# First block of a two-block transformer: HGRN levels on half the queries, weight splits on VectorE, padding zeros on GpSimdE

## The chip, the cores and the metric

One Trainium2 chip, one of its cores. The metric is device time of one execution in microseconds (us); lower is better. Times of before: median of three runs. Engines: TensorE (PE; its weight loads PEld), VectorE (DVE), ScalarE (ACT), GpSimdE (POOL), and SyncE (SP), which issues most DMAs.

## The reference, cut to what matters

Two residual blocks over 512 tokens of 1024 features, all in float32. The first has three mixers side by side (stick-breaking attention with 8 heads, an HGRN recurrence with 4 heads, memory attention with 4 heads), an output product, and a mixture of 16384 small experts (PEER). The second has three dilated-window groups and a memory attention. The change is in the first block's mixers; in the second it touches one pair of weights. The HGRN recurrence of a head is

```
f = lb + (1 - lb) * sigmoid(f_logit);  k = 1 - f;  b = cumsum(log f)
score[t, s] = sum_d q[t, d] * exp(b[t, d] - b[s, d]) * k[s, d]      for s <= t
out = score @ v  +  (q * exp(b)) @ state;   state = exp(b_last) * state + (k * exp(b_last - b))^T @ v
```

## The kernel before

**Weights.** A float32 product is made of three products of a faster TensorE type. Each weight tile of 128 x 2048 (8 chunks of 128 input features by 256 outputs) comes by two DMAs as `w_raw`; ScalarE rounds each half to `w_hi` (L110), and a second engine makes the rest, `w_lo = w_raw - w_hi` (L111, two SBUF operands of 1024 elements a partition, called a split below). `mm_feat` (L124 to L126) and `mm_tok` (L134 to L136) multiply hi*hi, hi*lo, lo*hi. `w_hi` and `w_lo` have two buffers, `w_raw` three. `weight(..., nc.gpsimd)` puts the splits of the first block's projections (`feat`, `tok`, `mem_kv`: 15 weights, 30 splits) and of `mem_kv_2` (2 weights) on POOL; `w_out` and everything later use DVE, but for 16 splits of the first `scores` pass of PEER, which stay on POOL before and after.

**HGRN.** `hgrn_head` works on one head at a time, keys and queries with features on partitions, 512 tokens along the row. Within a chunk of 128 tokens the scores come level by level (L = 64, 32, ..., 1): in each group of 2L tokens the queries of the upper half meet the keys of the lower half, with decays taken from the middle of the group. Per level: two subtractions on DVE (L351, L352) into `hg_d`, one exponential on ACT (L353), zeros in the unused halves of `hg_qt` and `hg_kt` by POOL (L355, L356), two products on DVE (L357, L358), four 128 x 128 x 128 float32 products on PE (L342; each is two records in the trace) and one predicated copy of 128 x 512 into the scores `hg_sc` (L359). Seven levels, four heads: 28 of each.

**Other names.** `stick` is the stick-breaking attention: per block of keys `sb_a` (scores), `sb_sp` (softplus, L300), `sb_h`/`sb_l` (its split, L304), a cumulative sum on PE (L306 to L309, tile `att`), L311, an exponential, and the values (L317, tile `acc`). `zero_pads` (L233, L234) clears the unused halves of padded queries. `norm_rows` and `head_rms` form a mean square, then one power on POOL (L97), then a multiplication (L163 for rows, L321 and L526 for heads).

**Order.** A scheduler orders every engine's instructions at build time, from the program's order and data dependences; at run time each engine takes its own list strictly in order. The two stick halves and four HGRN heads are interleaved with the products of the projections, which are the work that PE has at hand while DVE works through the levels.

Of the kernel before, what the change touches and what calls it, by code (L numbers as in the profile page):

```python
# [9 lines left out]
F32 = mybir.dt.float32  # L10
# [6 lines left out]
OP = mybir.AluOpType  # L17
# [3 lines left out]
S, D, P = 512, 1024, 128  # L21
NB = S // P
# [65 lines left out]
class Body:  # L88
# [96 lines left out]
    def mem_kv(self, xt, kT, v, pool, wpool, psm, pst):  # L185

        nc = self.nc
        wk = self.weight("w_mem_kv", 0, wpool, 2, nc.gpsimd)
        wv = self.weight("w_mem_kv", 1, wpool, 2, nc.gpsimd)
        ks = []  # L190
        for b in range(2):
            ps = psm.tile([P, 512], F32, name="mm")
            self.mm_tok(ps[:, :256], wk, xt, b * P)
            r = self.head_rms(ps[:, :256], 4, pool)
            kn = pool.tile([P, 4, 64], F32, name="ma_a", bufs=2)
            nc.vector.tensor_tensor(kn, ps[:, :256].rearrange("p (h d) -> p h d", d=64),
                                    r[:, :, None].to_broadcast([P, 4, 64]), op=OP.mult)
            ks.append(kn.rearrange("p h d -> p (h d)"))
        for b in range(2):
            ps = psm.tile([P, 512], F32, name="mm")  # L200
            self.mm_tok(ps[:, :256], wv, xt, b * P)
            nc.vector.tensor_copy(v[:, b, :], ps[:, :256])
        for c in range(2):
            ps = pst.tile([P, 512], F32, name="tp")
            for b in range(2):
                nc.tensor.transpose(ps[:, b * P:(b + 1) * P], ks[b][:, c * P:(c + 1) * P], self.ident)
            nc.scalar.activation(kT[:, c, :], ps[:, :256], AF.Copy, scale=self.vec[:, V_MK:V_MK + 1])

    def mem_kv_2(self, xt, kT, v, wpool, psm):

        nc = self.nc
        wk, wv = (self.weight("w_mem_kv_2", i, wpool, 2, nc.gpsimd) for i in range(2))
        yield
        for c in range(2):
            ps = psm.tile([P, 512], F32, name="mm")
            self.mm_feat(ps[:, :256], wk, xt, c * P)
            nc.scalar.activation(kT[:, c, :], ps[:, :256], AF.Copy)
        for b in range(2):
            ps = psm.tile([P, 512], F32, name="mm")
            self.mm_tok(ps[:, :256], wv, xt, b * P)  # L220
            nc.vector.tensor_copy(v[:, b, :], ps[:, :256])
        yield
# [101 lines left out]
    def hgrn_head(self, h, q, k, vi, mixed, pool, phg, pst):  # L324

        nc = self.nc
        T = lambda n, bufs=1: pool.tile([P, S], F32, name=n, bufs=bufs)
        v4 = lambda t: t.rearrange("p (c q) -> p c q", c=4)
        b, d = T("hg_b", 2), T("hg_d", 2)
        lb, oml, moml = (self.lbv[:, n, h:h + 1] for n in range(3))  # L330
        nc.scalar.activation(d, k, AF.Ln, bias=lb, scale=oml)
        for c in range(NB):
            sl = slice(c * P, (c + 1) * P)
            nc.vector.tensor_tensor_scan(b[:, sl], self.rst, d[:, sl], 0.0, op0=OP.mult, op1=OP.add)
        nc.vector.tensor_scalar(k, k, moml, oml, op0=OP.mult, op1=OP.add)
        sc = T("hg_sc", 2)

        def scores(kt, qt):
            pd = phg.tile([P, 512], F32, name="hs")
            for c in range(NB):  # L340
                sl = slice(c * P, (c + 1) * P)
                nc.tensor.matmul(pd[:, sl], kt[:, sl], qt[:, sl], start=True, stop=True)  # L342
            return v4(pd)

        nc.vector.tensor_tensor(v4(sc), scores(k, q), self.ident[:, None, :].to_broadcast([P, 4, P]), op=OP.mult)
        for n, L in enumerate(LEVELS):
            bl = lambda t: t.rearrange("p (n l) -> p n l", l=2 * L)
            bb = bl(b)
            mid = bb[:, :, L - 1:L].to_broadcast([P, S // (2 * L), L])
            d = T("hg_d", 2)  # L350
            nc.vector.tensor_tensor(bl(d)[:, :, L:], bb[:, :, L:], mid, op=OP.subtract)  # L351
            nc.vector.tensor_tensor(bl(d)[:, :, :L], mid, bb[:, :, :L], op=OP.subtract)  # L352
            nc.scalar.activation(d, d, AF.Exp)  # L353
            qt, kt = T("hg_qt", 2), T("hg_kt", 2)
            nc.gpsimd.memset(bl(qt)[:, :, :L], 0.0)  # L355
            nc.gpsimd.memset(bl(kt)[:, :, L:], 0.0)  # L356
            nc.vector.tensor_tensor(bl(qt)[:, :, L:], bl(d)[:, :, L:], bl(q)[:, :, L:], op=OP.mult)  # L357
            nc.vector.tensor_tensor(bl(kt)[:, :, :L], bl(d)[:, :, :L], bl(k)[:, :, :L], op=OP.mult)  # L358
            nc.vector.copy_predicated(v4(sc), self.hmask[:, n, :][:, None, :].to_broadcast([P, 4, P]), scores(kt, qt))  # L359

        d = T("hg_d", 2)
        nc.vector.tensor_tensor(v4(d), v4(b)[:, :, P - 1:P].to_broadcast([P, 4, P]), v4(b), op=OP.subtract)
        nc.scalar.activation(d, d, AF.Exp)
        kt = T("hg_kt", 2)
        nc.vector.tensor_tensor(kt, d, k, op=OP.mult)
        nc.scalar.activation(b, b, AF.Exp)
        qd = T("hg_qt", 2)
        nc.vector.tensor_tensor(qd, b, q, op=OP.mult)
        vsl = slice(h // 2 * P, h // 2 * P + P)
# [54 lines left out]
    def first(self, cp, gp, xr):  # L424
        nc, tc, A = self.nc, self.tc, self.A
        with ExitStack() as es:
# [24 lines left out]
            def tok(i, dst):
                w = self.weight("w_in", i, wpool, 2, nc.gpsimd)
# [8 lines left out]
            def hgrn_in(pair):  # L461
# [2 lines left out]
                feat(6 + pair, both[:, 0])  # L464
                return both[:, 0], both[:, 1]

            vi = pool.tile([P, NB, 256], F32, name="hg_i")
            rows = []
            for n in range(2):
# [814 lines left out]
```

## Time and profile before

| | us |
|---|---|
| median of three runs | 1969.91 (1967.43 to 1970.49) |
| the profiled execution | 1971.19 |
| its span in the trace | 1969.4 |
| first block, to the last addition of `w_out` (L585) | about 393 |

The profiled execution is 1.3 us above the median; the trace covers all of it but 1.8 us. A wait "<- X" after an instruction names what ended the idle time of its engine just before it. Busy times of PE are modelled and overlap a little, so its waits are more telling than its share.

### The profile page before, as it was taken

What the parts mean: (1) busy time and instruction counts of PE and PEld (TensorE: products, weight loads), DVE (VectorE), ACT (ScalarE), POOL (GpSimd) and SP (SyncE); (2) the same over time, 40 slices, a digit from 0 to 9 for tenths busy, and PEclk for the clock granted to TensorE, in tenths of its full rate; (3) what the DMA queues carried; (4) which work ended last, traced back from release to release, by engine and by line L of the source; (5) the groups of instructions that cost most, each with busy time, mean ns of one, the idle gap of its engine ahead of it and who ended that gap; (6) DMA issues with size and microseconds to landing.
All of it is one profiled execution on the core that took longest, in us unless ns stands there. A gap on an engine that the chain in (4) does not pass through costs nothing.

```text
span 1969.4 us, 29893 instructions
## 1 busy us (share of the span) xinstructions
PE 1873.6 (95%) x11285; PEld 1703.4 (86%) x11285; DVE 1403.8 (71%) x2718; ACT 866.7 (44%) x1363; POOL 562.0 (29%) x479
## 2 busy tenths in 40 slices
PE   7899888989889989999999999999999799999998
PEld 6778787989889989999998999999998678889898
DVE  3387886369999979767876877787787675433563
ACT  4474745155569654333333433343333433443442
POOL 4323322070000000034443544455444332113100
PEclk9999998999999999999999999999999999999999
DMA  4211102454457686778999999989998775422221
GB/s 159 84 47 61 44 22 67 148 163 142 148 177 268 208 288 186 235 262 311 339 319 314 311 340 328 330 304 334 323 318 308 275 255 186 149 73 89 76 65 54
DMA packets 150769, 399.25 MB, mean 203 GB/s; under 512 B 12768, under 2 KB 62048, under 8 KB 147552
## 3 DMA queue, kind: packets, MB, share of 16 engines
q1 hardware_dynamic: 110688, 257.30, 39.4%
q0 software_dynamic: 39360, 137.94, 19.5%
q8 instruction: 88, 1.44, 0.3%
q10 hardware_dynamic: 576, 2.10, 0.3%
q14 instruction: 57, 0.47, 0.1%
HBM read 364.75 MB, written 30.41 MB: 201 GB/s over the span
## 4 chain that ended last, share of the span: by engine, by line
PE 59%; DVE 13%; issue 7%; DMA 6%; POOL 3%; ACT 2%; POOLq 0%; DVEq 0%; SPq 0%; ACTq 0%
PE o L720 20%; PE hp L624 7%; PE hp L626 7%; PE hp L625 7%; PE mm L134 3%; PE mm L136 3%; PE mm L135 3%; DVE w_lo L111 2%; DMA g_row<-peer_u,idx 2%; DMA g_row<-peer_v,idx 2%; DVE onehot L913 2%; DMA w_raw<-peer_v 1%; PE mm L124 1%; PE mm L125 1%; PE mm L126 1%
## 5 line engine op out<-in xcount | busy, mean ns | idle before, releaser
L110 ACT ACTIVATE w_hi<-w_raw 128x1024 fp32r<-128x1024 f32 x366 | 386.1, 1060 | 576.4 <-DMA w_raw<-peer_v 199.2
L111 DVE TENSOR_TENSOR w_lo<-w_raw,w_hi 128x1024 fp32r<-128x1024 f32 x316 | 384.4, 1219 | 103.3 <-ACT w_hi L110 97.3
L624 PE MATMUL hp<-xT_hi,w_hi 128*128 128x384 f32 x1024 | 350.2, 342 | 0.4 <-ACT act L630 0.4
L626 PE MATMUL hp<-xT_hi,w_lo 128*128 128x384 f32 x1024 | 347.6, 339 | 2.5 <-DVE w_lo L111 2.5
L625 PE MATMUL hp<-xT_lo,w_hi 128*128 128x384 f32 x1024 | 346.8, 339 | 0.0
L954 POOL DMA_INDIRECT g_row<-peer_u,idx x128 | 172.9, 1351 | 339.1 <-PE o L720 137.7
L720 PE MATMUL o<-w_hi,wl 128*128 128x512 f32 x768 | 240.2, 394 | 8.8 <-DVE wl L715 8.8
L720 PE MATMUL o<-w_hi,wh 128*128 128x512 f32 x768 | 241.1, 396 | 7.4 <-ACT wh L714 7.4
L720 PE MATMUL o<-w_lo,wh 128*128 128x512 f32 x768 | 239.5, 393 | 0.0
L954 POOL DMA_INDIRECT g_row<-peer_v,idx x128 | 174.0, 1359 | 222.6 <-PE o L720 149.2
L958 DVE SCALAR_TENSOR_TENSOR g_row<-g_row,kv 128x1024 f32<-128x1024 f32 x128 | 155.2, 1222 | 68.3 <-DMA g_row<-peer_u,idx 67.9
L624 PEld LDWEIGHTS hp<-xT_hi,w_hi 128*128 128x128 f32 x1024 | 193.2, 189 | 4.4 <-ACT act L630 0.8
L625 PEld LDWEIGHTS hp<-xT_lo,w_hi 128*128 128x128 f32 x1024 | 193.1, 189 | 3.6
L626 PEld LDWEIGHTS hp<-xT_hi,w_lo 128*128 128x128 f32 x1024 | 193.4, 189 | 3.1 <-DVE w_lo L111 3.1
L720 PEld LDWEIGHTS o<-w_hi,wl 128*128 128x128 f32 x768 | 145.5, 190 | 41.1 <-DVE wl L715 10.9
L720 PEld LDWEIGHTS o<-w_lo,wh 128*128 128x128 f32 x768 | 146.0, 190 | 32.0
L720 PEld LDWEIGHTS o<-w_hi,wh 128*128 128x128 f32 x768 | 144.4, 190 | 31.3 <-ACT wh L714 8.2
L963 DVE SCALAR_TENSOR_TENSOR x<-g_row,dots,x 128x1024 f32<-128x1024 f32 x100 | 128.3, 1283 | 48.9 <-DMA g_row<-peer_v,idx 48.5
L714 ACT ACTIVATE wh<-act 128x384 fp32r<-128x384 f32 x128 | 66.7, 522 | 203.7 <-PE o L720 192.6
L111 POOL TENSOR_TENSOR w_lo<-w_raw,w_hi 128x1024 fp32r<-128x1024 f32 x50 | 121.0, 2431 | 104.2 <-ACT w_hi L110 101.0
L125 PE MATMUL mm<-xT_lo,w_hi 128*128 128x256 f32 (+1 forms) x400 | 129.5, 324 | 0.0
L124 PE MATMUL mm<-xT_hi,w_hi 128*128 128x256 f32 (+1 forms) x384 | 127.2, 332 | 0.6 <-ACT xT_hi L153 0.6
(351 smaller groups left out, 3634.4 us busy)
## 6 DMA issues: line engine op xcount, KB each, us to landing
w_raw<-peer_uT SPq DMA_DIRECT2D x128, 512.0 KB
w_raw<-peer_v SPq DMA_DIRECT2D x128, 512.0 KB
w_raw<-w_in SPq DMA_DIRECT2D x54, 512.0 KB
gd<-stage SPq DMA_DIRECT2D x23, 1024.0 KB
gt<-gd SPq DMA_DIRECT2D x15, 1536.0 KB
w_raw<-w_query SPq DMA_DIRECT2D x32, 512.0 KB
w_raw<-w_out SPq DMA_DIRECT2D x16, 512.0 KB
w_raw<-w_mem_kv SPq DMA_DIRECT2D x8, 512.0 KB
```

Source lines behind the costliest of these rows:

```text
L110: nc.scalar.activation(hi[:, sl], raw, AF.Copy)
L111: eng.tensor_tensor(lo[:, sl], raw, hi[:, sl].bitcast(F32), op=OP.subtract)
L124: nc.tensor.matmul(ps, a, xh[:, kc, :], start=kc == 0, stop=False)
L125: nc.tensor.matmul(ps, a, xl[:, kc, :], start=False, stop=False)
L624: nc.tensor.matmul(ps, uh[:, kc, :], hi[:, kc, P:], start=kc == 0, stop=False)
L625: nc.tensor.matmul(ps, uh[:, kc, :], lo[:, kc, P:], start=False, stop=False)
L626: nc.tensor.matmul(ps, ul[:, kc, :], hi[:, kc, P:], start=False, stop=kc == KC - 1)
L714: nc.scalar.activation(wh, w, AF.Copy)
L720: last = nc.tensor.matmul(out[b][n], s_[:, sl], m_[:, n * 512:(n + 1) * 512], start=i == 0 and m_ is vh and s_ is wh, stop=i == NE - 1 and ...
L954: dma = nc.gpsimd.indirect_dma_start(out=u, out_offset=None, in_=A["peer_v" if k >= P else "peer_u"], in_offset=bass.IndirectOffsetOnAxis( ...
L958: nc.vector.scalar_tensor_tensor(u, u, 1.0, self.h2, op0=OP.mult, op1=OP.mult, accum_out=dots[:, c:c + 1])
L963: nc.vector.scalar_tensor_tensor(y, u, dots[:, c:c + 1], x, op0=OP.mult, op1=OP.add)
```

## The change

HGRN: the queries of the upper halves are packed into 256 columns (`hg_qt` of 128 x 256), the decays of queries and keys lie in the two halves of `hg_d`, the four products of a level move 64 columns instead of 128, and the predicated copy covers 256 elements (the late half of each group). `hg_kt` becomes two fixed tiles, cleared once; what a former level left in their other halves falls on rows that the mask doesn't copy. The 56 small memsets of POOL go. The last key product of a head is written over `hg_d`, and `hg_qe` takes the decayed queries. All 34 splits of POOL in `feat`, `tok`, `mem_kv` and `mem_kv_2` go to DVE (30 in the first block, 4 in the second). The padding zeros of the first stick half go from DVE to POOL.

```
-        wk = self.weight("w_mem_kv", 0, wpool, 2, nc.gpsimd)
+        wk = self.weight("w_mem_kv", 0, wpool)
...
-            nc.vector.tensor_tensor(bl(d)[:, :, L:], bb[:, :, L:], mid, op=OP.subtract)
-            nc.vector.tensor_tensor(bl(d)[:, :, :L], mid, bb[:, :, :L], op=OP.subtract)
+            nc.vector.tensor_tensor(half(d[:, :256]), bb[:, :, L:], mid, op=OP.subtract)
+            nc.vector.tensor_tensor(half(d[:, 256:]), mid, bb[:, :, :L], op=OP.subtract)
             nc.scalar.activation(d, d, AF.Exp)
-            qt, kt = T("hg_qt", 2), T("hg_kt", 2)
-            nc.gpsimd.memset(bl(qt)[:, :, :L], 0.0)
-            nc.gpsimd.memset(bl(kt)[:, :, L:], 0.0)
-            nc.vector.tensor_tensor(bl(qt)[:, :, L:], bl(d)[:, :, L:], bl(q)[:, :, L:], op=OP.mult)
-            nc.vector.tensor_tensor(bl(kt)[:, :, :L], bl(d)[:, :, :L], bl(k)[:, :, :L], op=OP.mult)
-            nc.vector.copy_predicated(v4(sc), self.hmask[:, n, :][:, None, :].to_broadcast([P, 4, P]), scores(kt, qt))
+            qt = pool.tile([P, 256], F32, name="hg_qt", bufs=2)
+            nc.vector.tensor_tensor(half(qt), half(d[:, :256]), bl(q)[:, :, L:], op=OP.mult)
+            kt = self.kts[n % 2]
+            nc.vector.tensor_tensor(bl(kt)[:, :, :L], half(d[:, 256:]), bl(k)[:, :, :L], op=OP.mult)
+            pd = phg.tile([P, 512], F32, name="hs")[:, :256]
+            for c in range(NB):
+                nc.tensor.matmul(pd[:, c * 64:(c + 1) * 64], kt[:, c * P:(c + 1) * P], qt[:, c * 64:(c + 1) * 64],
+                                 start=True, stop=True)
+            nm = P // (2 * L)
+            late = v4(sc).rearrange("p c (n l) -> p c n l", l=2 * L)[:, :, :, L:]
+            mask = self.hmask[:, n].rearrange("p (n l) -> p n l", l=2 * L)[:, :, L:]
+            nc.vector.copy_predicated(late, mask[:, None].to_broadcast([P, 4, nm, L]),
+                                      pd.rearrange("p (c n l) -> p c n l", c=4, l=L))
...
-                w = self.weight("w_in", i, wpool, 2, nc.gpsimd)
+                w = self.weight("w_in", i, wpool)
...
+            self.kts = [pool.tile([P, S], F32, name=f"hg_kt{n}") for n in range(2)]
+            for t in self.kts:
+                nc.gpsimd.memset(t, 0.0)
...
-            def stick_in(eng, g):
+            def stick_in(g):
...
-                self.zero_pads(qz, eng)
+                self.zero_pads(qz, nc.gpsimd)
```

The scheduler sets a new order. Three places of it, as the built programs have them. The first is DVE in the first levels of the third head. Before:

```order
L501 TENSOR_TENSOR hg_qf<-hg_qf,hg_d 128x512
L300 SCALAR_TENSOR_TENSOR sb_sp<-sb_a,sb_sp 128x512
L357 TENSOR_TENSOR hg_qt<-hg_d,hg_qf 128x4x64
L358 TENSOR_TENSOR hg_kt<-hg_d,hg_qf 128x4x64
L351 TENSOR_TENSOR hg_d<-hg_b 128x8x32
L304 TENSOR_TENSOR sb_l<-sb_sp,sb_h 128x512
L352 TENSOR_TENSOR hg_d<-hg_b 128x8x32
L351 TENSOR_TENSOR hg_d<-hg_b 128x16x16
L295 COPY sb_a<-att 128x512
L311 TENSOR_TENSOR sb_a<-sb_a,att 128x512
L357 TENSOR_TENSOR hg_qt<-hg_d,hg_qf 128x8x32
L345 TENSOR_TENSOR hg_sc<-hs,cst 128x512
```

And POOL, at the same place before (the two splits belong to the next weights):

```order
L97 TENSOR_TENSOR hr_r_1691<-rs_t,mhalf 128x4
L111 TENSOR_TENSOR w_lo<-w_raw,w_hi 128x1024 x2
L355 MEMSET hg_qt 128x16x16
L356 MEMSET hg_kt 128x16x16
L355 MEMSET hg_qt 128x32x8
L356 MEMSET hg_kt 128x32x8
```

DVE at the same place of the change (L349, L350 are the subtractions, L353 and L356 the products, L364 the predicated copy):

```order
L341 TENSOR_TENSOR hg_sc<-hs,cst 128x512
L300 SCALAR_TENSOR_TENSOR sb_sp<-sb_a,sb_sp 128x512
L353 TENSOR_TENSOR hg_qt<-hg_d,hg_qf 128x256
L356 TENSOR_TENSOR hg_kt_103<-hg_d,hg_qf 128x4x64
L353 TENSOR_TENSOR hg_qt<-hg_d,hg_qf 128x256
L356 TENSOR_TENSOR hg_kt_104<-hg_d,hg_qf 128x8x32
L349 TENSOR_TENSOR hg_d<-hg_b 128x256
L364 COPY_PREDICATED hg_sc<-hmask,hs 128x4x64
L304 TENSOR_TENSOR sb_l<-sb_sp,sb_h 128x512
L350 TENSOR_TENSOR hg_d<-hg_b 128x256
```

No split of a weight stands between this head's levels; the four of the two weights in question stand ahead of the head. In all four heads together, four splits stand between the first subtraction and the last predicated copy of a head (1, 2, 0 and 1). The second place is DVE at the start of the first stick half, before:

```order
L456 COPY sb_v<-mm 128x256 x4
L293 TENSOR_TENSOR sb_a<-att,cst 128x512
L300 SCALAR_TENSOR_TENSOR sb_sp<-sb_a,sb_sp 128x512
L304 TENSOR_TENSOR sb_l<-sb_sp,sb_h 128x512
L311 TENSOR_TENSOR sb_a<-sb_a,att 128x512
```

and in the change:

```order
L462 COPY sb_v<-mm 128x256 x4
L293 TENSOR_TENSOR sb_a<-att,cst 128x512
L111 TENSOR_TENSOR w_lo<-w_raw,w_hi 128x1024 x2
L300 SCALAR_TENSOR_TENSOR sb_sp<-sb_a,sb_sp 128x512
L304 TENSOR_TENSOR sb_l<-sb_sp,sb_h 128x512
L311 TENSOR_TENSOR sb_a<-sb_a,att 128x512
```

Two splits moved in between L293 and L300, where DVE waits for three passes of ACT over `sb_sp`. The third place is POOL at the program's start, before:

```order
L97 TENSOR_TENSOR rs<-rs_t,mhalf 128x1 x4
L111 TENSOR_TENSOR w_lo<-w_raw,w_hi 128x1024
L233 MEMSET sb_qz 64x2x512
L111 TENSOR_TENSOR w_lo<-w_raw,w_hi 128x1024
L234 MEMSET sb_qz 64x2x512
L111 TENSOR_TENSOR w_lo<-w_raw,w_hi 128x1024 x10
```

and in the change:

```order
L97 TENSOR_TENSOR rs<-rs_t,mhalf 128x1 x2
L233 MEMSET sb_qz 64x2x512
L97 TENSOR_TENSOR rs<-rs_t,mhalf 128x1
L234 MEMSET sb_qz 64x2x512
L97 TENSOR_TENSOR rs<-rs_t,mhalf 128x1
L233 MEMSET sb_qz 64x2x512
L234 MEMSET sb_qz 64x2x512
L97 TENSOR_TENSOR hr_r_612<-rs_t,mhalf 128x4
```

The first padding zeros now stand between the powers of the second, third and fourth block of rows, and no split is left among them. From the PEER stage on, the lists of all engines are the same but for the four splits of `mem_kv_2` and a few neighbours.

## Rows read from the trace of the kernel before

**Rows 1.** Page, busy time, share of the span and instructions of each engine.

```profile
PE 1873.6 (95%) x11285; PEld 1703.4 (86%) x11285; DVE 1403.8 (71%) x2718; ACT 866.7 (44%) x1363; POOL 562.0 (29%) x479
```

**Rows 2.** Waits of PE from 60 to 300 us: total us, times, longest.

```profile
PE hs L342 <- DVE hg_kt L358: 12.1, 5, 3.9
PE att L307 <- DVE sb_l L304: 3.4, 3, 1.6
PE acc L317 <- ACT sb_a L312: 2.2, 3, 1.4
PE att L306 <- ACT sb_h L303: 1.7, 1, 1.7
```

**Rows 3.** The same view from 300 to 345 us.

```profile
PE tp L530 <- DVE xrow L526: 2.8, 1, 2.8
```

**Rows 4.** Timeline around 220 us: start, us, engine, instruction, [idle before].

```profile
219.69 1.05 PE L342 MATMUL hs<-hg_qf 128*128 128x128 f32 x8
...
219.99 4.86 POOL L111 TENSOR_TENSOR w_lo<-w_raw,w_hi 128x1024 fp32r<-128x1024 f32 x2 [10.01 <-ACT w_hi L110]
220.26 2.38 DVE L357 TENSOR_TENSOR hg_qt<-hg_d,hg_qf 128x256 f32<-128x256 f32 x1
...
223.17 1.96 DVE L358 TENSOR_TENSOR hg_kt<-hg_d,hg_qf 128x256 f32<-128x256 f32 x1
...
225.28 0.91 PE L342 MATMUL hs<-hg_qt,hg_kt 128*128 128x128 f32 x6 [3.18 <-DVE hg_kt L358]
```

**Rows 5.** Groups of DVE by shape, 60 to 300 us: busy us, mean ns.

```profile
L359 DVE COPY_PREDICATED hg_sc<-hmask,hs 128x512 f32<-128x512 uint8 x28 | 20.5, 734 | 2.1 <-PE hs L342 2.0
L304 DVE TENSOR_TENSOR sb_l<-sb_sp,sb_h 128x512 fp32r<-128x512 f32 x20 | 17.2, 861 | 2.9 <-ACT sb_h L303 2.8
L357 DVE TENSOR_TENSOR hg_qt<-hg_d,hg_qf 128x256 f32<-128x256 f32 x28 | 17.0, 608 | 0.4 <-ACT hg_d L353 0.3
L358 DVE TENSOR_TENSOR hg_kt<-hg_d,hg_qf 128x256 f32<-128x256 f32 x28 | 16.6, 594 | 0.0
L300 DVE SCALAR_TENSOR_TENSOR sb_sp<-sb_a,sb_sp 128x512 f32<-128x512 f32 x20 | 15.6, 779 | 8.8 <-ACT sb_sp L299 8.6
L351 DVE TENSOR_TENSOR hg_d<-hg_b 128x256 f32<-128x256 f32 x28 | 13.9, 496 | 0.0
...
L352 DVE TENSOR_TENSOR hg_d<-hg_b 128x256 f32<-128x256 f32 x28 | 11.7, 417 | 0.0
...
L365 DVE TENSOR_TENSOR hg_kt<-hg_d,hg_qf 128x512 f32<-128x512 f32 x4 | 2.7, 676 | 0.0
```

**Rows 6.** Busy us (instructions) of the splits L111 from 60 to 300 us.

```profile
60.00:300.00 240.00, 0.00 (x0) 49.12 (x21) 0.99 0.16 50
```

**Rows 7.** Groups of DVE by shape, 300 to 395 us.

```profile
L111 DVE TENSOR_TENSOR w_lo<-w_raw,w_hi 128x1024 fp32r<-128x1024 f32 x8 | 9.6, 1220 | 1.3 <-ACT w_hi L110 1.3
```

**Rows 8.** Busy us of all engines and granted clock (PEclk) in two stretches.

```profile
60.00:300.00 240.00, 215.57 (x1321) 185.71 (x1319) 179.09 (x355) 135.65 (x222) 80.00 (x89) 0.99 0.16 50
300.00:340.00 40.00, 35.03 (x220) 30.16 (x221) 27.84 (x65) 22.65 (x54) 8.76 (x7) 0.87 0.22 72
```

**Rows 9.** Timeline of the start of the program.

```profile
10.48 0.75 DVE L163 TENSOR_SCALAR xrow<-sb_qz,rs 128x1024 f32<-128x1024 f32 x1 [0.67 <-POOL rs L97]
...
11.57 0.91 DVE L233 MEMSET sb_qz<- 64x1024 f32 x1 [0.27 <-DVE rs_t L96]
...
13.92 2.34 POOL L111 TENSOR_TENSOR w_lo<-w_raw,w_hi 128x1024 fp32r<-128x1024 f32 x1
...
14.32 2.49 DVE L163 TENSOR_SCALAR xrow<-sb_qz,rs 128x1024 f32<-128x1024 f32 x1
...
18.10 0.75 DVE L154 SCALAR_TENSOR_TENSOR xT_lo<-att,vec,xT_hi 128x512 fp32r<-128x512 f32 x1 [1.29 <-ACT xT_hi L153]
```

**Rows 10.** Timeline of PE, one run of half-precision products in the PEER stage.

```profile
601.55 0.64 PE L922 MATMUL g<-gated,onehot 128*128 128x128 f16 x8
```

**Rows 11.** Waits of ACT from 18 to 300 us.

```profile
ACT w_hi L110 <- PE mm L136: 13.5, 3, 8.5
```

More of the change, by code (lines that the diff above doesn't have):

```diff
@@ L187, in mem_kv @@
         nc = self.nc
-        wk = self.weight("w_mem_kv", 0, wpool, 2, nc.gpsimd)
-        wv = self.weight("w_mem_kv", 1, wpool, 2, nc.gpsimd)
+        wk = self.weight("w_mem_kv", 0, wpool)
+        wv = self.weight("w_mem_kv", 1, wpool)
         ks = []
@@ L211, in mem_kv_2 @@
         nc = self.nc
-        wk, wv = (self.weight("w_mem_kv_2", i, wpool, 2, nc.gpsimd) for i in range(2))
+        wk, wv = (self.weight("w_mem_kv_2", i, wpool) for i in range(2))
         yield
@@ L336, in hgrn_head @@
         sc = T("hg_sc", 2)
[L338 to L345, printed above, removed]
+        pd = phg.tile([P, 512], F32, name="hs")
+        for c in range(NB):
+            sl = slice(c * P, (c + 1) * P)
+            nc.tensor.matmul(pd[:, sl], k[:, sl], q[:, sl], start=True, stop=True)
+        nc.vector.tensor_tensor(v4(sc), v4(pd), self.ident[:, None, :].to_broadcast([P, 4, P]), op=OP.mult)
         for n, L in enumerate(LEVELS):
             bl = lambda t: t.rearrange("p (n l) -> p n l", l=2 * L)
+            half = lambda t: t.rearrange("p (n l) -> p n l", l=L)
             bb = bl(b)
@@ L350, in hgrn_head @@
             d = T("hg_d", 2)
-            nc.vector.tensor_tensor(bl(d)[:, :, L:], bb[:, :, L:], mid, op=OP.subtract)
-            nc.vector.tensor_tensor(bl(d)[:, :, :L], mid, bb[:, :, :L], op=OP.subtract)
+            nc.vector.tensor_tensor(half(d[:, :256]), bb[:, :, L:], mid, op=OP.subtract)
+            nc.vector.tensor_tensor(half(d[:, 256:]), mid, bb[:, :, :L], op=OP.subtract)
             nc.scalar.activation(d, d, AF.Exp)
-            qt, kt = T("hg_qt", 2), T("hg_kt", 2)
-            nc.gpsimd.memset(bl(qt)[:, :, :L], 0.0)
-            nc.gpsimd.memset(bl(kt)[:, :, L:], 0.0)
-            nc.vector.tensor_tensor(bl(qt)[:, :, L:], bl(d)[:, :, L:], bl(q)[:, :, L:], op=OP.mult)
-            nc.vector.tensor_tensor(bl(kt)[:, :, :L], bl(d)[:, :, :L], bl(k)[:, :, :L], op=OP.mult)
-            nc.vector.copy_predicated(v4(sc), self.hmask[:, n, :][:, None, :].to_broadcast([P, 4, P]), scores(kt, qt))
+            qt = pool.tile([P, 256], F32, name="hg_qt", bufs=2)
[3 more added lines that the diff above has]
+            pd = phg.tile([P, 512], F32, name="hs")[:, :256]
+            for c in range(NB):
+                nc.tensor.matmul(pd[:, c * 64:(c + 1) * 64], kt[:, c * P:(c + 1) * P], qt[:, c * 64:(c + 1) * 64],
[5 more added lines that the diff above has]
+                                      pd.rearrange("p (c n l) -> p c n l", c=4, l=L))
         d = T("hg_d", 2)
@@ L363, in hgrn_head @@
         nc.scalar.activation(d, d, AF.Exp)
-        kt = T("hg_kt", 2)
+        kt = d
         nc.vector.tensor_tensor(kt, d, k, op=OP.mult)
         nc.scalar.activation(b, b, AF.Exp)
-        qd = T("hg_qt", 2)
+        qd = T("hg_qe")
         nc.vector.tensor_tensor(qd, b, q, op=OP.mult)
@@ L451, in tok @@
             def tok(i, dst):
-                w = self.weight("w_in", i, wpool, 2, nc.gpsimd)
+                w = self.weight("w_in", i, wpool)
                 for b in range(NB):
@@ L552, in first @@
             tok(10, slabs(vi))
-            sb = stick_in(nc.vector, 0)
+            sb = stick_in(0)
             self.masks(cp, pool.tile([P, len(LEVELS) + 2, P], F32, name="hg_qf", bufs=1))
@@ L558, in first @@
             hgrn(0, *hin)
-            sb = stick_in(nc.gpsimd, 1)
+            sb = stick_in(1)
             hgrn(1, *hin)
```

## Prediction

> **What bounds the kernel now.** The page's first part comes first [rows 1]: PE is busy 95% of the span, DVE 71%, POOL 29%. So a gain has to come from PE's work or from PE's waits, not from busy time of DVE or POOL as such. The change lies in the first block, which ends near 393 us, so PE's waits there are read next, in the stretch of stick attention and HGRN heads from 60 to 300 us [rows 2]. Four kinds make 12.1 + 3.4 + 2.2 + 1.7 = 19.4 us, and one more of 2.8 us comes right behind [rows 3]: 22.2 us in all. Each ends on a DVE result, or on an ACT result that waited for one. In the same 240 us DVE is busy for 179.1 us, three quarters [rows 8], so it is not a shortage of DVE that PE waits for, but single late instructions.
>
> The timeline around 220 us shows why they are late [rows 4]. Two splits run on POOL from 219.99 to 224.85 us. L357, a product of 128 x 256 with both operands in SBUF, starts at 220.26 and lasts 2.38 us, until the first split ends; L358 starts at 223.17 and lasts 1.96 us, until the second ends. PE stood idle for 3.18 us and went on at 225.28 us. The means by shape say the same over the whole stretch [rows 5]: L352 (128 x 256, two SBUF operands) takes 417 ns, but L357 608, L358 594 and L351 496 at the same size; L365 (128 x 512) takes 676 ns, but L304 861 and L300 779. I read this as POOL's split and a DVE instruction with two SBUF operands not running side by side: the later one stands until the other is through. The stands add up to 20 x (0.861 - 0.676) + 20 x (0.779 - 0.676) + 28 x (0.608 - 0.417 + 0.594 - 0.417 + 0.496 - 0.417) = 3.7 + 2.1 + 12.5 = 18.3 us, beside PE's 19.4 us of waits: a stand on DVE goes through to PE nearly whole, since it strikes whichever instruction is next.
>
> **The change, part by part.** All sums are against the profiled execution, 1971.2 us.
>
> *The splits leave POOL.* The stands go with them, and with them PE's waits [rows 2, 3]: -22.2 us. At the least nothing is gained, if something else holds DVE as long (a rival below); more than the 22.2 is not there in these rows.
>
> *The splits arrive on DVE.* In the stretch 21 of them [rows 6] at 1.22 us [rows 7] make 25.6 us. On the other side DVE sheds the 18.3 us of stands, and the shorter predicated copies: no row has one of 256 elements, so I take the step between the unhindered products, 676 - 417 = 259 ns [rows 5], 28 times, 7.3 us (between nothing and half of 20.5, 10.3 us). 25.6 - 18.3 - 7.3 = 0: DVE has as much to do as before, in another order. What counts is who stands behind a split. By the new order, four of them stand between the levels of the four heads, where the next products of PE come from; the others stand ahead of a head, behind its last level, or where DVE has a wait for ACT anyway (8.6 us in L300's row [rows 5] are such waits). I let the four go through whole, 4 x 1.22 = +4.9 us; the bounds are 0 and all 21 of them, +25.6 us. Within the levels the packed operands have the same element counts for the subtractions and products, so they are taken at no change; POOL's 56 memsets were hidden behind other engines' work, and their end is taken at nothing.
>
> *The start.* The last block of rows, L163, lasted 2.49 us beside POOL's first split, an earlier one 0.75 [rows 9]: a stand of 1.74 us, with PE's first products behind it. I take 1.5 of it. Two zero-paddings of 0.91 us leave DVE's list between these rows and go to POOL, between its powers; that is a swap on the same chain and taken at nothing (bounds: 2 x 0.91 = 1.8 us either way). The first split now stands on DVE in front of the first L154, which waited 1.29 us for ACT anyway [rows 9], against 1.22 us. Sum -1.5 us, between -1.74 - 1.8 = -3.5 and +1.8.
>
> *The clock.* The granted clock is 0.99 in the long stretch and 0.87 from 300 to 340 us [rows 8]; the missing pulses are worth 0.01 x 240 + 0.13 x 40 = 2.4 + 5.2 = 7.6 us. The trace has the lower of the two levels, 1.2 GHz, in such stretches and 2.4 GHz else, and the fall comes behind gaps like that of [rows 4]. If the gaps go, part of it comes back; but 300 to 340 us has waits of its own (for powers and row sums) that stay. I take -3 us, between 0 and -7.6.
>
> *PE's products of the levels.* 112 products of 128 moving columns get 64. Each is two records, and eight records follow each other at 0.111 us (1.05 us for the eight at 219.69 us less a tail of about 0.28 us, by seven steps [rows 4]). If the step halves, 224 x 0.056 = 12.5 us of PE work go; if the weight load sets it, nothing does, since every product still loads 128 weights. No row has fewer than 128 moving columns. The nearest row with cheaper columns is L922, half precision at 128 columns: eight in 0.64 us [rows 10], about 0.06 us a step, but its weights are half precision too, so it does not tell the two apart. I take the bound nothing: the float32 steps in the trace never fall under this one. The Trainium skill has a rule that speaks against a gain here, in "TensorE: Matmul & The Clock Gate", section "LDWEIGHTS (loading the stationary operand)": a load takes the weight columns divided by 1.2, in ns, whatever is streamed behind it. By that rule, as an estimate, 128 columns cost 107 ns a record, next to the measured 0.111 us, and the term is 0; with the halved step of the same page's "Back-to-back issue gap" it would be -12.5 us.
>
> *The second block.* The four splits of `mem_kv_2` cost DVE 4 x 1.22 = 4.9 us where there is PE work of other weights at hand, and free it of at most as many stands of about 2 us. Taken at nothing, between +4.9 and -4 us, for want of a wait of PE that names them.
>
> Sum: -22.2 + 4.9 - 1.5 - 3 = -21.8 us, 1949.4 us for a profiled execution. That one stood 1.3 us over its median, so **1948 us**. The PEER stage behind starts when the last row of x is added and keeps its order, so it moves as a whole.
>
> **Rivals.**
>
> *DVE is simply the next to be late.* DVE's busy time does not change (25.6 us in, 25.6 us out). If splits hold PE as the stands did, us for us, only the start is gained: 1969.9 - 1.5 = 1968 us, no change. For it: from 100 to 300 us the levels are one chain on DVE, and a list in strict order can't let a level pass a split. Against: a quarter of DVE's time is free [rows 8], and the stands struck at random while the splits have places.
>
> *A split blocks its list.* A split on DVE waits for `w_hi`, and ACT can't write `w_hi` before PE is through with the weights of two tiles ago: that made ACT wait 13.5 us in three places, 8.5 us at the longest [rows 11]. On POOL nobody stood behind such a wait but memsets and powers; on DVE all levels do. 21 splits belong to about 11 weights. At the mean wait of 4.5 us each, on seven of them, 31.5 us come on top of 1948: 1980 us, slower. It decides from about 26 us, 2.3 us a weight. Against: the scheduler knows these dependences and puts the splits behind the products in question, and PE has to reach the same weights later anyway.
>
> *The halved products count.* 12.5 us less on PE, in a stretch that PE fills: 1935 us. It is the rule of the issue gap against that of the load, above.
>
> **How the numbers follow.** This kernel's measurement tells about 0.2%, 4 us, from no change (1966 to 1974 us). Chances: the forecast, 1938 to 1958 us, 0.55; the halved products or more clock, below 1938, 0.15; splits that cost PE most of what is gained, 1958 to 1974, 0.22, of which 0.12 lie under 1966; the blocked list, over 1974, 0.08. Faster 0.82, the same 0.10, slower 0.08. The range that leaves out about 2 in 10 reaches from 1929 (the halved products and the whole clock: 1948 - 12.5 - 4.6 = 1931, and a little of the start) to 1967 us; the likeliest case's own is 1938 to 1958.
>
> **What would show it.** Right: in the new trace L353, L356, L304 and L300 (its line before) have means near 0.42 and 0.68 us; PE's waits for them in the stretch to 300 us fall from 19 us to under 7; DVE's busy time there is the same within 5 us in a shorter stretch; the records of the level products still follow at 0.11 us. The first rival shows as PE waits of the same sum ending on the same DVE lines, now with L111 in front of them; the second as DVE idle in front of L111 for ACT; the third as a step near 0.06 us. The prediction is wrong if PE's waits go but the end of the block does not move, which would say that something other than PE's list bounds it.

## The result and the profile after

The changed kernel takes **1953.15 us** (median of 6 runs, 1947.34 to 1955.3), the kernel before 1969.51 us beside it (6 runs, 1967.12 to 1971.2). The ratio is 0.9926, 95% interval 0.9909 to 0.9944: 0.74% faster, 14.6 us by the ratio. The forecast was 1948 us with a range of 1929 to 1967. The profiled execution took 1954.04 us with a span of 1952.3, 17.1 us less than before.

The page of the changed kernel, busy time of each engine, answers to [rows 1]. POOL has lost its splits (562.0 to 474.5 us) and DVE has gained only 4.2 us, although it took them over:

```profile
PE 1867.4 (96%) x11285; PEld 1702.6 (87%) x11285; DVE 1408.0 (72%) x2750; ACT 864.5 (44%) x1363; POOL 474.5 (24%) x393
```

PE's waits from 60 to 300 us in the changed kernel (total us, times, longest) answer to [rows 2]. L359 is L342 before:

```profile
PE mm L134 <- DVE ma_a L196: 3.2, 1, 3.2
PE att L307 <- DVE sb_l L304: 2.2, 4, 0.9
...
PE hs L359 <- DVE hg_kt L356: 0.8, 1, 0.8
...
PE att L306 <- ACT sb_h L303: 0.3, 1, 0.3
PE acc L317 <- ACT sb_a L312: 0.3, 1, 0.3
```

The four kinds of [rows 2] made 19.4 us; the same four make 2.2 + 0.8 + 0.3 + 0.3 = 3.6 us now. The longest wait of the levels' products, 3.9 us, is gone.

DVE's groups by shape over the same stretch (busy us, mean ns, then the idle time before them) answer to [rows 5]; L353 and L356 are the level products L357 and L358 of before, L349 the subtraction L351, L364 the predicated copy L359:

```profile
L111 DVE TENSOR_TENSOR w_lo<-w_raw,w_hi 128x1024 fp32r<-128x1024 f32 x22 | 26.7, 1222 | 3.5 <-ACT w_hi L110 3.5
L364 DVE COPY_PREDICATED hg_sc<-hmask,hs 128x256 f32<-128x256 uint8 x28 | 14.8, 527 | 4.3 <-PE hs L359 4.0
L300 DVE SCALAR_TENSOR_TENSOR sb_sp<-sb_a,sb_sp 128x512 f32<-128x512 f32 x20 | 13.8, 688 | 5.5 <-ACT sb_sp L299 5.4
L304 DVE TENSOR_TENSOR sb_l<-sb_sp,sb_h 128x512 fp32r<-128x512 f32 x20 | 13.7, 685 | 0.7 <-ACT sb_h L303 0.7
...
L356 DVE TENSOR_TENSOR hg_kt<-hg_d,hg_qf 128x256 f32<-128x256 f32 x28 | 11.8, 422 | 0.0
L353 DVE TENSOR_TENSOR hg_qt<-hg_d,hg_qf 128x256 f32<-128x256 f32 x28 | 11.8, 420 | 0.6 <-ACT hg_d L351 0.5
...
L349 DVE TENSOR_TENSOR hg_d<-hg_b 128x256 f32<-128x256 f32 x28 | 11.7, 418 | 0.0
```

The reader is to see the means: 608, 594 and 496 ns have become 420, 422 and 418; 861 and 779 have become 685 and 688. That is the mean of an instruction that nothing holds. The splits' idle time before them, 3.5 us for ACT, is all that the blocked list (a rival) came to in this stretch.

To put the gain on one scale I take the same instruction in both traces, PE's first transpose of the memory keys (L206), which starts at 317.2 us before and at 296.4 us after: a lead of 20.8 us. The busy time of each engine (PE, PEld, DVE, ACT, POOL; granted clock behind them) in the first 60 us and from 60 us to it, before:

```profile
0.00:60.00 60.00, 46.34 (x265) 40.53 (x266) 16.65 (x34) 24.69 (x34) 28.04 (x24) 1.00 0.43 147
...
60.00:317.20 257.20, 229.98 (x1426) 199.71 (x1424) 187.83 (x374) 144.65 (x238) 84.06 (x92) 0.98 0.16 51
```

and after, with the second stretch of [rows 8] as its last line:

```profile
0.00:60.00 60.00, 47.51 (x272) 41.70 (x273) 25.52 (x42) 24.64 (x34) 7.13 (x14) 1.00 0.45 157
...
60.00:296.40 236.40, 225.00 (x1422) 198.68 (x1421) 181.68 (x398) 143.95 (x239) 21.47 (x20) 0.99 0.18 56
...
300.00:340.00 40.00, 35.73 (x255) 31.97 (x254) 21.66 (x49) 15.88 (x43) 1.01 (x1) 0.96 0.32 106
```

PE's idle time fell from 257.2 - 230.0 = 27.2 us to 236.4 - 225.0 = 11.4, by 15.8 us, and its busy time by 5.0. The work is not quite the same, since the changed kernel is further on at 60 us: by then PE has been busy 47.51 - 46.34 = 1.2 us longer. So the 20.8 us are 15.8 of idle time, 1.2 from the first 60 us, and 5.0 - 1.2 = 3.8 by which the same products take less time. The changed kernel keeps its lead of 20.8 us until the last addition of `w_out` on DVE (392.86 us before, 372.07 after), and then loses part of it. ACT's list, at the place where the first block hands over to PEER (L596, before L587, stores a finished row of x, L160 squares it for PEER's norm), before:

```profile
384.60 0.34 ACTq L587 DMA_DIRECT2D x<-xrow  x1
385.00 1.06 ACT L160 ACTIVATE h2r<-xrow 128x1024 f32<-128x1024 f32 x1 [13.24 <-DVE xrow L585]
```

and after:

```profile
363.99 6.02 ACTq L596 DMA_DIRECT2D x<-xrow  x3
370.11 1.06 ACT L160 ACTIVATE h2r<-xrow 128x1024 f32<-128x1024 f32 x1 [18.81 <-DVE xrow L594]
```

and DVE's list there, after:

```profile
372.07 0.42 DVE L594 TENSOR_TENSOR xrow<-xrow,mm 128x256 f32<-128x256 f32 x1 [2.42 <-PE mm L136]
...
373.29 0.75 DVE L163 TENSOR_SCALAR h2r<-xrow,rs 128x1024 f32<-128x1024 f32 x1 [0.74 <-POOL rs L97]
...
380.51 2.82 DVE L163 TENSOR_SCALAR h2r<-xrow,rs 128x1024 f32<-128x1024 f32 x1 [0.66 <-POOL rs L97]
383.25 2.44 DVE L625 CAST t_iota<-cst 128x256 f16<-128x256 f32 x1
```

Three stores, each of which waits for its row of x, stand in front of the first square; before, squares and stores took turns. So only one square starts ahead of the last addition, where it was three before, and all four row scalings (L163) come behind it, where two came ahead of it before. The cast of `t_iota`, which follows the norm on DVE, starts 11.18 us behind the last addition; before, it was 3.48 us. Some of that is made good in PEER: 17.1 us of the 20.8 reach the end of these two executions.

### The profile page after: what moved, and what is told of

Read it like the earlier page. It is cut to its first block, busy times and chain, and to the rows that moved or that the text cites. A ratio compares the mean times of both kernels' runs of the same rounds, so it can differ in the third digit from the quotient of the medians.

```text
span 1952.3 us, 29773 instructions
## 1 busy us (share of the span) xinstructions
PE 1867.4 (96%) x11285; PEld 1702.6 (87%) x11285; DVE 1408.0 (72%) x2750; ACT 864.5 (44%) x1363; POOL 474.5 (24%) x393
## 4 chain that ended last, share of the span: by engine, by line
PE 73%; DVE 12%; issue 6%; DMA 3%; ACT 3%; POOL 3%; POOLq 0%; SPq 0%; DVEq 0%; ACTq 0%
PE o L729 21%; PE hp L633 8%; PE hp L635 8%; PE hp L634 8%; PE mm L134 4%; PE mm L136 4%; PE mm L135 4%; PE mm L125 3%; PE mm L126 3%; PE mm L124 3%; DVE w_lo L111 2%; DMA g_row<-peer_v,idx 2%; DVE onehot L922 2%; PE hs L359 1%; POOL g_row L963 1%
## 5 line engine op out<-in xcount | busy, mean ns | idle before, releaser
L111 DVE TENSOR_TENSOR w_lo<-w_raw,w_hi 128x1024 fp32r<-128x1024 f32 x350 | 425.5, 1219 | 123.8 <-ACT w_hi L110 123.3
L963 POOL DMA_INDIRECT g_row<-peer_v,idx x128 | 178.7, 1396 | 214.1 <-PE o L729 135.5
L126 PE MATMUL mm<-xT_hi,w_lo 128*128 128x256 f32 (+1 forms) x384 | 124.5, 325 | 0.2 <-DVE w_lo L111 0.2
```

Of the source, the lines that this page charges most:

```text
L111: eng.tensor_tensor(lo[:, sl], raw, hi[:, sl].bitcast(F32), op=OP.subtract)
L126: nc.tensor.matmul(ps, b, xh[:, kc, :], start=False, stop=kc == KC - 1)
L963: dma = nc.gpsimd.indirect_dma_start(out=u, out_offset=None, in_=A["peer_v" if k >= P else "peer_u"], in_offset=bass.IndirectOffsetOnAxis( ...
```

## The experiments

The changed kernel differs from the one before in three things that can be had apart: where the splits run, how the levels are packed, and where in tile memory the kept pair of zeroed key tiles lies. The last is a side effect. The pair comes from the first pool, ahead of the weight tiles, and pushes them up by 4,096 bytes a partition; in the built program (no trace shows addresses) the third raw weight tile then lies at bytes 82,784 to 86,880, and the first row tile of PEER's norm (`h2r`, which takes the space over) at 85,344 to 89,440. Before, the raw tiles ended at 82,784. A square that writes into that row tile has to wait for the last use of the last raw weight tile, and the order of ACT's list was laid down accordingly.

**Splits alone.** The kernel before, with this change only (the same for all weights of `w_in`, `w_mem_kv` and `w_mem_kv_2`):

```
-        wk = self.weight("w_mem_kv", 0, wpool, 2, nc.gpsimd)
+        wk = self.weight("w_mem_kv", 0, wpool)
...
-                w = self.weight("w_in", i, wpool, 2, nc.gpsimd)
+                w = self.weight("w_in", i, wpool)
```

> The kernel before with one part of the change: all weight splits of w_in, w_mem_kv and w_mem_kv_2 on VectorE; levels, pads and tile sizes as before. Theory (POOL's splits and DVE's instructions with two SBUF operands hold each other; the splits carry the gain): PE's waits from 60 to 300 us fall from 19 us to under 8, the last row of w_out is added about 16 to 20 us earlier than before, and since the tile sizes are those of before, the handover to PEER keeps its old order and nothing is lost there: 1948 to 1954 us. Rival (the packed levels carry the gain, since they shorten the predicated copies and drop 56 memsets): 1964 to 1970 us.

Measured: 1943.1 us (6 runs) beside 1964.05 us of before on that chip, ratio **0.9889** (0.9870 to 0.9909), 21.9 us of 1969.5. PE's waits from 60 to 300 us:

```profile
PE acc L317 <- ACT sb_a L312: 2.4, 3, 1.4
PE hs L342 <- DVE hg_kt L358: 2.3, 2, 1.4
PE att L307 <- DVE sb_l L304: 1.7, 3, 0.7
...
PE att L306 <- ACT sb_h L303: 0.2, 1, 0.2
```

With a fourth of 0.2 us these are 6.6 us, where the four of [rows 2] made 19.4. The last addition of `w_out` comes 22.7 us earlier, more than the 16 to 20 expected. The splits carry the gain, and more than the whole change brings.

**Levels alone.** The changed kernel with the edits above taken back, and the first pads back on DVE.

> The changed kernel with the splits back on POOL and the first pads back on VectorE, so that only the packed levels, with their kept pair of zeroed tiles, are left of the change. Theory: DVE still stands behind POOL's splits; the shorter predicated copies (5.8 us less work on DVE) bring at most some 5 us, and the larger first pool costs the about 6 us at the handover to PEER that the changed kernel showed: 1964 to 1974 us. Rival (the levels carry the gain): 1948 to 1956 us.

Measured: 1972.15 us (12 runs), ratio **1.0033** (1.0019 to 1.0048): slower than before. DVE still stands behind POOL's splits; PE's waits from 60 to 300 us:

```profile
PE hs L359 <- DVE hg_kt L356: 7.2, 5, 2.8
PE att L307 <- DVE sb_l L304: 4.8, 4, 1.5
PE att L306 <- ACT sb_h L303: 4.3, 2, 2.5
PE acc L317 <- ACT sb_a L312: 2.9, 3, 1.4
```

They make 19.2 us, against 19.4. The stands hit other instructions, but as hard. The loss, 6.5 us by the ratio, is a little more than the expectation allowed (1974 us beside 1969.5).

**The kept tiles elsewhere.** The changed kernel, and only the place of the pair moved:

```
-            self.kts = [pool.tile([P, S], F32, name=f"hg_kt{n}") for n in range(2)]
-            for t in self.kts:
-                nc.gpsimd.memset(t, 0.0)
             vi = pool.tile([P, NB, 256], F32, name="hg_i")
...
             stick(0, sb)
+            self.kts = [tp.tile([P, S], F32, name=f"hg_kt{n}") for n in range(2)]
+            for t in self.kts:
+                nc.gpsimd.memset(t, 0.0)
             hin = hgrn_in(0)
```

> The changed kernel with one thing moved: the kept pair of zeroed key tiles is taken from the pool of working tiles, just before the first HGRN pair, not from the pool that lies ahead of the weights. In the changed kernel the third raw weight tile lies over the first row tile of PEER's norm, so that the first square of that norm stands behind the whole of w_out, and with it three stores of x1 stand ahead of it. Theory (that overlap costs the handover about 6 us): the order there is again that of before, ScalarE's squares between the stores, and the time falls to 1945 to 1949 us. Rival (the lead shrinks at the handover for another reason, such as work that is not of the first block and does not move with it): 1951 to 1955 us, as the changed kernel.

Measured: 1945.86 us (6 runs), ratio **0.9902** (0.9884 to 0.9921), against 0.9926 of the changed kernel. The two intervals overlap, and 0.9902 of 1969.5 us is 1950.2, between what the theory and the rival expected; by its time alone this run settles nothing. ACT's list at the handover has stores and squares in turn again:

```profile
363.56 0.34 ACTq L596 DMA_DIRECT2D x<-xrow  x1
363.95 1.06 ACT L160 ACTIVATE h2r<-xrow 128x1024 f32<-128x1024 f32 x1 [13.08 <-DVE xrow L594]
```

The first square starts at 363.95 instead of 370.11 us, with the last addition at the same time (372.13 and 372.07). The next run shows the cost by itself.

**The overlap without the change.** The kernel before, with its own `hg_kt` buffers taken from the first pool and nothing else:

```
-            qt, kt = T("hg_qt", 2), T("hg_kt", 2)
+            qt, kt = T("hg_qt", 2), self.p1.tile([P, S], F32, name="hg_kt", bufs=2)
```

> The kernel before with nothing of the change but one tile's place: the two buffers of hg_kt, written and used as before, are taken from the first pool, ahead of the weights, instead of the pool of working tiles, so that the raw weight tiles lie 4 kB per partition higher, as in the changed kernel, and the third lies over the first row tile of PEER's norm. Theory (the overlap by itself costs the handover 5 to 7 us): the first block ends as before, and the time is 5 to 7 us over before, a ratio of 1.0025 to 1.0036. Rival (the handover is shorter of slack only when the first block is faster): within 2 us of before.

Measured: 1972.74 us (12 runs), ratio **1.0028** (1.0017 to 1.0039), +5.5 us. The same two rows of ACT as in the changed kernel, 21 us later:

```profile
385.03 6.08 ACTq L588 DMA_DIRECT2D x<-xrow  x3
391.16 1.06 ACT L160 ACTIVATE h2r<-xrow 128x1024 f32<-128x1024 f32 x1 [18.98 <-DVE xrow L586]
```

**Levels alone, tiles kept in their pool.** The run of the levels alone, and the pair of tiles placed as in the run with the kept tiles elsewhere.

> As e2_levels_only, with the pair of zeroed key tiles in the pool of working tiles, as in e3. Theory (packed levels are worth nothing by themselves, and e2's loss was the handover's): within 3 us of before, a ratio of 0.9985 to 1.0015. Rival (packed levels disturb the first block itself): as e2, 1.002 and more.

Measured: 1965.76 us (12 runs), ratio **0.9986** (0.9972 to 1.0000). So packing by itself is worth about 0.14%, between nothing and 0.28%, and the loss of the levels alone was the handover's.

The handover can be read by itself in each trace: from the last addition of `w_out` to the first cast of PEER's selected indices (`tf`), in us.

| kernel | ratio to before | last addition | `tf` | between |
|---|---|---|---|---|
| before | 1 | 392.86 | 465.62 | 72.8 |
| changed | 0.9926 | 372.07 | 450.02 | 78.0 |
| splits alone | 0.9889 | 370.16 | 442.29 | 72.1 |
| levels alone | 1.0033 | 392.20 | 470.89 | 78.7 |
| levels alone, tiles kept | 0.9986 | 389.62 | 460.92 | 71.3 |
| changed, kept tiles elsewhere | 0.9902 | 372.13 | 443.82 | 71.7 |
| before, tile moved | 1.0028 | 393.21 | 471.89 | 78.7 |

Where the tiles overlap it takes 78.0 to 78.7 us, elsewhere 71.3 to 72.8, whatever the first block does. From `tf` to the end these single executions take 1494 to 1504 us, so what happens behind it can't be told from one trace.

**Idle work on POOL.** As the run with the kept tiles elsewhere, and behind each of the first 22 splits:

```
             eng.tensor_tensor(lo[:, sl], raw, hi[:, sl].bitcast(F32), op=OP.subtract)
+            if self.idle is not None:
+                nc.gpsimd.tensor_tensor(self.idle, lo[:, sl].bitcast(F32), lo[:, sl].bitcast(F32), op=OP.mult)
```

> As e3_kept_tiles_elsewhere, and behind each of the first 22 splits, which stay on VectorE, POOL multiplies the finished low part with itself into a tile that is not in use yet (128x1024, float32, two operands in SBUF): work that nobody reads and nobody waits for; the lists of VectorE and TensorE are word for word those of e3. Theory (a POOL operation with two SBUF operands and a DVE operation of that kind hold each other): DVE's means of the level products and of the low parts rise again from 0.42 and 0.68 us, with single ones of 2 us and more beside POOL's work, and 8 to 20 us come back: 1953 to 1966 us. Rival (the splits were late on POOL, because POOL takes 2.4 us for what DVE does in 1.2, and the stands on DVE cost nothing by themselves): within 3 us of e3.

Measured: 1956.52 us (6 runs) beside 1967.68, ratio **0.9946** (0.9933 to 0.9960): 0.9946 - 0.9902 = 0.44%, 8.7 us, of which the two intervals allow 4 to 13. The last addition of `w_out` comes at 382.73 us, 10.6 later. The timeline from 68 us (PE and ACT left out):

```profile
68.69 5.04 POOL L115 TENSOR_TENSOR hg_g<-w_lo 128x1024 f32<-128x1024 f32 x2 [7.18 <-DVE w_lo L113]
...
69.75 2.23 DVE L304 SCALAR_TENSOR_TENSOR sb_sp<-sb_a,sb_sp 128x512 f32<-128x512 f32 x1
...
72.68 1.60 DVE L308 TENSOR_TENSOR sb_l<-sb_sp,sb_h 128x512 fp32r<-128x512 f32 x1 [0.70 <-ACT sb_h L307]
```

the same place without the idle work (L300 and L304 are L304 and L308 above):

```profile
69.24 0.69 DVE L300 SCALAR_TENSOR_TENSOR sb_sp<-sb_a,sb_sp 128x512 f32<-128x512 f32 x1
...
70.64 0.69 DVE L304 TENSOR_TENSOR sb_l<-sb_sp,sb_h 128x512 fp32r<-128x512 f32 x1 [0.70 <-ACT sb_h L303]
```

and, with the idle work again, two of DVE's groups by shape from 60 to 300 us:

```profile
L304 DVE SCALAR_TENSOR_TENSOR sb_sp<-sb_a,sb_sp 128x512 f32<-128x512 f32 x20 | 16.9, 847 | 4.8 <-ACT sb_sp L303 4.7
...
L315 DVE TENSOR_TENSOR sb_a<-sb_a,att 128x512 f32<-128x512 f32 x20 | 13.6, 681 | 1.7 <-PE att L311 1.4 <-PE att L313 0.2
```

Nobody reads what POOL makes, DVE's and PE's lists are the same as without it, and yet 0.69 us have become 2.23 and 1.60, and a bit under half of the 0.98% gained is lost again. From 60 to 300 us the idle work is 27.6 us, where the splits before were 49. That is the theory's sign, at the lower end of its size. Not all of it is holding: the power of a row norm stands behind two idle operations in POOL's own list, DVE waits for it 3.9 us instead of 0.7, and across that wait its lag behind the run without idle work grows from 7.7 to 8.8 us. That is about 1 of the 10.6 us. The mean of L315, whose second operand is in PSUM, stays at 681 ns; the one that started while an idle operation ran, at 121.70 us, took 0.68 us. The level products stay as they were, since no idle operation ran beside one; the expectation had named them.

Two operands in SBUF are not needed on DVE's side. A TENSOR_SCALAR of 128 x 1024 (L184), which reads one tile, took 2.39 us beside POOL's idle work, against 0.69 without; before, it is L180 and stood behind a split:

```profile
90.12 2.87 DVE L180 TENSOR_SCALAR hg_qf<-hg_qf 128x1024 f32<-128x1024 f32 x1
```

The row scalings (L163, one tile and a number per row) and the cast of `t_iota` (one tile) were held as well.

**The same with one operand.** `tensor_scalar` in place of POOL's `tensor_tensor`.

> As e4_idle_pool_work, but POOL's idle operation has one operand in SBUF (the low part times a constant, into the same tile). Theory A (only POOL's operations with two SBUF operands hold DVE): within 3 us of e3, DVE's means as in e3. Theory B (any long POOL operation on SBUF does, as the zeroing beside a row scaling of 1.41 against 0.75 us at the start suggests): DVE's stands as in e4_idle_pool_work, and a time between e3's and e4's, by the length of POOL's operation.

Measured: 1954.55 us (6 runs), ratio **0.9932** (0.9917 to 0.9947), 5.9 us over the run without idle work (1 to 11 by the intervals). The timeline at the same place:

```profile
68.26 3.61 POOL L115 TENSOR_SCALAR hg_g<-w_lo 128x1024 f32<-128x1024 f32 x1 [5.22 <-DVE w_lo L113]
...
69.31 1.38 DVE L304 SCALAR_TENSOR_TENSOR sb_sp<-sb_a,sb_sp 128x512 f32<-128x512 f32 x1
...
71.38 0.69 DVE L308 TENSOR_TENSOR sb_l<-sb_sp,sb_h 128x512 fp32r<-128x512 f32 x1 [0.69 <-ACT sb_h L307]
```

POOL is busy longer, and yet L304 stands for 0.7 us only and L308 not at all. Theory B is right that one operand is enough; the stands are shorter, not as in the run before. The 5.9 us are not theirs alone. DVE's waits have the same power behind two idle operations:

```profile
DVE sb_v L167 <- POOL rs L99: 5.7, 1, 5.7
```

Without idle work this wait is 0.7 us. Across it DVE's lag grows from 3.1 to 5.9 us, of 6.5 at the last addition, so nearly half of the loss is POOL's own list being longer. Against the run with two operands the times are too close to be told apart.

**Splits done twice.** As the run with the kept tiles elsewhere, each split of `w_in` and `w_mem_kv` repeated on DVE.

> As e3_kept_tiles_elsewhere, and each split of w_in and w_mem_kv is done twice on VectorE, with the same result: some 21 times 1.22 us (25.6 us) more DVE work in the stretch from 60 to 300 us. It doses the term of the splits that arrive on DVE. Theory (a quarter of DVE's time is free there, four splits lie among the levels): 3 to 9 us above e3. Rival (DVE is the next to be late, us for us): 20 to 28 us above e3.

Measured: 1955.76 us (6 runs), ratio **0.9935** (0.9919 to 0.9952): 0.33%, 6.5 us over the run with single splits (2 to 11). The last addition comes 8.2 us later (380.36). The splits on DVE up to 400 us:

```profile
L114 DVE TENSOR_TENSOR w_lo<-w_raw,w_hi 128x1024 fp32r<-128x1024 f32 x68 | 81.9, 1219 | 16.9 <-ACT w_hi L112 16.6
```

With single splits they are 38 and 46.0 us. The expectation counted only the stretch from 60 to 300 us; over the first block there are 30 further splits. These 35.9 us of DVE work cost about a fifth of themselves (6.5 us by the ratio, 8.2 by the last addition). The rival (us for us) is out. The scheduler set a new order here too, so the run measures the dose together with its order.

**Two splits of `w_query` on DVE too**, with the packed levels and without:

```
-... WB, None if between else nc.gpsimd, 1)]
+... WB, None if between or i < 2 else nc.gpsimd, 1)]
```

> As e3_kept_tiles_elsewhere, and the first two splits of w_query, which stand on POOL beside the last row of PEER's norm, are on VectorE. Theory: the last row's scaling (2.82 us beside POOL's split, 0.75 alone) gets shorter by about 2 us and the handover with it: 1 to 2.5 us under e3. Rival (two splits of 1.22 us on VectorE stand in front of the first low parts there and take it back): within 1 us of e3 or above it.

> The kernel before with the splits of w_in, w_mem_kv, w_mem_kv_2 and the first two of w_query on VectorE, levels untouched: the parts that helped, together. Theory: e1's ratio of 0.989 or 1 to 2 us better, 0.987 to 0.989 of before. Rival (the two splits of w_query bring nothing): as e1, 0.989 to 0.991.

Measured: 1942.42 us (6 runs), ratio **0.9883** (0.9865 to 0.9902), with the levels; 1944.45 us (5 runs), ratio **0.9881** (0.9865 to 0.9898), without. Both are 0.1 to 0.2% under the runs without this edit, which the intervals do not separate. The traces hint at it: from last addition to `tf` it is 69.9 and 70.4 us. The place was not the one I named. Once the tiles are elsewhere the last row's scaling is free already (0.75 us), and it is the cast behind it that POOL's first split held. With the kept tiles elsewhere alone:

```profile
375.62 2.44 DVE L625 CAST t_iota<-cst 128x256 f16<-128x256 f32 x1
```

and with the two splits on DVE:

```profile
377.38 0.29 DVE L625 CAST t_iota<-cst 128x256 f16<-128x256 f32 x1
```

These two kernels have the lowest ratios of the study, 1.2% under the kernel before, but are not told apart from the splits alone.

## Why the prediction was right, and where it was not

**The bound and the mechanism were right.** PE waited for single DVE instructions that stood behind POOL's splits. The splits alone give 0.9889; POOL work that nobody reads brings the stands and 0.44% of the time back, about 1 us of it by way of POOL's own list. So the holding itself costs time. The Trainium skill says as much in "SBUF — State Buffer", section "Who interferes with whom": a DVE instruction with two inputs in SBUF contends with a POOL instruction that reads SBUF, and the one that is issued second waits. The idle POOL work agrees: 2.23 and 1.60 us with two inputs in SBUF, 0.68 with one in PSUM. The prediction's condition, two SBUF operands on DVE, was too narrow: instructions that read one tile stood as long (L180, 2.87 us). Of DVE's two-port modes the same section of the Trainium skill says that the first has the shared ports for the whole instruction; two-operand POOL work looks like that here, but beside one-operand work L304 was through at 70.69 us, while POOL's operation ran until 71.87. What it is worth by itself that the splits come earlier on DVE was not measured apart.

**The splits leave and arrive** (-22.2 + 4.9 = -17.3 us). Measured to the same instruction, PE's idle time fell by 15.8 us. The stay-behind was put at 4.9. The doubled splits measured 8.2 us in the first block; DVE was already 4.4 us late at 60 us, so some 4 fall into the stretch, for about the dose that the prediction had there. In the largest wait left, 3.2 us for `ma_a`, 0.9 us show that holding goes both ways. In the changed kernel:

```profile
286.48 1.23 DVE L111 TENSOR_TENSOR w_lo<-w_raw,w_hi 128x1024 fp32r<-128x1024 f32 x1
...
286.64 1.93 POOL L97 TENSOR_TENSOR hr_r<-rs_t,mhalf 128x4 f32<-128x4 f32 x1 [9.98 <-DVE rs_t L96]
...
290.24 1.01 POOL L97 TENSOR_TENSOR hr_r<-rs_t,mhalf 128x4 f32<-128x4 f32 x1 [1.66 <-DVE rs_t L96]
```

A power on POOL, started beside a split on DVE, took 1.93 us instead of 1.01, and PE's products wait behind it; the rest of the 3.2 us is the chain of the norm itself.

**The start** (-1.5 us): 1.2 us of lead at PE's first products and in the first 60 us. The row scaling that lasted 2.49 us [rows 9] lasts 0.75; another now lasts 1.41 beside a zeroing on POOL.

**The clock** (-3 us): the same products took 3.8 us less of PE's busy time, and the granted clock from 60 us to L206 rose from 0.98 to 0.99. From 300 to 340 us it rose from 0.87 to 0.96, but there the changed kernel is 20 us further on. The sign and the order were right; what share of the 3.8 us is the clock's was not measured apart.

**The level products** (0): in the changed kernel's timeline of PE ten records of 128 x 64 take 1.23 us and six take 0.78, so one follows the other at 0.45 / 4 = 0.112 us, as at 128 columns.

```profile
112.49 0.78 PE L359 MATMUL hs<-hg_qt,hg_kt 128*128 128x64 f32 x6
...
116.72 1.23 PE L359 MATMUL hs<-hg_qt,hg_kt 128*128 128x64 f32 x10
```

Halving the moving columns gave nothing, as the runs of the levels alone say too. The third rival is out. The rule of "TensorE: Matmul & The Clock Gate", section "LDWEIGHTS (loading the stationary operand)", in the Trainium skill, agrees with that.

**Smaller sizes.** The predicated copy of 256 elements takes 527 ns, not 475. DVE's busy time from 60 us to the same instruction fell from 187.8 to 181.7 us, where I had it the same within 5: the sum of stands had left out four single ones (L180, L334, L526 and L96, together 7.6 us over their free time). The second block shows no change that could be told from the spread behind `tf`.

**The step that failed** is "The PEER stage behind starts when the last row of x is added and keeps its order, so it moves as a whole." It did not keep its order. I had followed which engine writes and reads the new pair of tiles, and not which bytes it takes. The sum of the terms to the end of the first block was -21.8 us, measured -20.8; then the handover took 5 to 6 us that no term had (78.0 us against 72.8 before and 71.7 with the tiles elsewhere). The tile's place by itself costs 0.28%; without it the changed kernel stands at 0.9902, which is 1950.2 us of 1969.5 and 2 us from the forecast. The other terms came out 1 us apart in sum (the splits 1.5 short, the start 0.3 short, PE's busy time 0.8 over), partly because errors of either sign offset each other.

## What to carry to other kernels

Before giving an engine work because it is idle, look in the timeline for instructions of its neighbour that last two to six times their usual time beside that work: here, with 49 us of splits moved from a POOL that was mostly free to a busier DVE, PE's idle time fell by some 16 us. An edit that adds or enlarges a tile moves all that lies behind it, and can put a late tile of one stage under an early tile of the next; look at the two lists at the next handover, and move the tile rather than the work. Try each part of a change alone: here one part carried more than the whole, one next to nothing, and one took a quarter back.

## What was not expected of the hardware

POOL's operation with one operand takes longer than that with two, and holds DVE less (0.7 us of L304 against 1.5). Why is open. POOL's groups by shape up to 300 us, of the run with one operand and of that with two:

```profile
L115 POOL TENSOR_SCALAR hg_g<-w_lo 128x1024 f32<-128x1024 f32 x22 | 65.2, 2964 | 84.5 <-DVE w_lo L113 83.9
```

```profile
L115 POOL TENSOR_TENSOR hg_g<-w_lo 128x1024 f32<-128x1024 f32 x22 | 45.8, 2081 | 99.5 <-DVE w_lo L113 99.2
```

And the holding is mutual: work moved from POOL to DVE delays what stays on POOL, here one of the powers that every norm waits for, by 0.9 us.
